# Modulations of two modules as elementwise sums in the feed-forward stage, scan projections spaced by a table, attention without bias tiles

## The chip, the core and the metric

The program runs on one core of a Trainium2 chip, as one launch. A core has a matrix engine (PE), a vector engine (DVE), an activation engine (ACT), a general engine (POOL) and a queue engine that mostly issues DMAs (SP). Each takes its own instructions strictly in order and waits on semaphores that other engines and DMAs raise; sixteen DMA engines move data between DRAM (HBM) and the on-chip memory. The metric is the device time of one execution in microseconds (us), lower is better. All data are float32.

## The reference, cut to what matters

Two blocks of layers run one after the other on 512 tokens of width 1024. Each of three modules needs six modulation vectors of 1024 numbers (shift, scale and gate, twice), made from one conditioning vector by a 1024 x 6144 matrix:

```python
for i in range(DEPTH):                      # first block: modules "0" and "1" of the kernel
    mod = silu(c) @ ada_w[i] + ada_b[i]     # (6144,), and the same for c_ctx
    sh1, sc1, gt1, sh2, sc2, gt2 = split(mod, 6)
    h = x * (1.0 + sc1) + sh1
    y = rwkv7_mixer(h, ...) if i == 0 else pool_mixer(h, ...)
    x = layer_norm(ALPHA * x + gt1 * y)
    h = x * (1.0 + sc2) + sh2
    y = swiglu(h, w1, w3, w2) if i == 0 else moe_swiglu(h, ...)
    x = layer_norm(ALPHA * x + gt2 * y)
# second block: module "2"
mod = silu(c_2) @ w_ada_2 + b_ada_2
h = h + gate1 * attention(modulate(rms_norm(h), shift1, scale1))   # scores + bias[key - query]
h = h + gate2 * conv_ffn(modulate(rms_norm(h), shift2, scale2))
```

The rwkv7 mixer holds a state per head that is updated token by token in both directions (a scan), first over 256 context tokens, then over the 512. The attention of the second block adds to the score of a query and a key a bias that depends on their distance alone.

## The kernel before, in words

The stages follow each other: features and projections of the rwkv7 mixer, its scan, its output projection with a normalisation, the SwiGLU feed-forward stage (hidden width 2816), the pooling mixer with the router, the expert stage, and the second block (attention, convolutional feed-forward).

A matmul in full precision is made of three. `part` splits a float32 tile into a rounded copy (`wh`, ACT, L166) and the remainder (`wl`, DVE, L167), and `mm3` (L172) multiplies high by high, high by low and low by high.

**The scan** (`phase_rwkv`) treats 16 heads as 8 pairs f = 0 to 7. A pair takes three passes of `chain(f, bt)` (L788 to L845): four chunks each, four steps per chunk, in which PE, ACT and DVE hand a 128 x 64 state to each other. `weave` runs a chain step by step and calls `fill` after each step: 48 steps per pair, 384 in all (and 13 before the first). Beside the chain it also runs pieces for the pairs that follow (`gram`, `inv`, `feats1`, `load_k`). `fill` advances the generator `background` by one step. Its steps are of two kinds. One is `job`: projections k, r and v of later pairs, 176 steps with up to six matmuls each (L934), whose results go to DRAM tiles (`kd_`, `rd_`, `vd`) and are read back by `load_k(f)` (L567) and its like. The other is `ada`: a chunk of 1024 columns of a module's modulation, a load of 128 x 1024 weights (512 KB, L228) per step, multiplied on PE with the silu of the conditioning vector as a 32-column stationary operand (L234), nine loads with the bias row, then a tenth step that copies, transposes (L241) and stores. Chunk by chunk, 16 chunks are made there: four of module "0" (its first two vectors are made earlier), six of "1", six of "2". They stand between the jobs from the second set of projections on; after the last job the generator goes on with the chunks that are left in 12 of 16 steps (`SPARE`). `bias_tiles` is called once per pair from the third on: a DMA that writes, for two bias heads, 128 shifted copies of a bias row (`k.bd`) into a DRAM tile `k.zd`.

**The feed-forward stage** (`phase_ffn`) goes over 22 blocks of 128 hidden columns in three groups of 8, 8 and 6 (`FCH`). For each pair of blocks two weight tiles of 1 MB are loaded (`load_w`, L154, four buffers `w`); for each block `glu` splits two 128-column parts of them (three buffers for `wh` and `wl`) and issues 2 x 24 matmuls. After a group `down` multiplies with `ffn_w2`, 192 matmuls for the first two groups; the last group's are spread over the pooling units that follow. Loads of weights are issued by SP, in order.

**Attention** reads for each of 12 bias heads a 128 x 896 tile `zr` from `k.zd` (`zload`, L1835), splits it and adds it to the scores by two matmuls with the identity `identr`.

The order of instructions on each engine is not that of the code: a scheduler places each instruction where its own timeline finds it ready, keeping the dependences. `tc.issue_after` ties a fill to the chain step before it.

## Time and profile before

| | |
|---|---|
| Time, median of 3 runs | 3094.28 us (3085.50 to 3096.80) |
| Profiled execution | 3069.05 us, its span 3067.3 us |
| Busy in the span | PE 2688.0 us (88%), DVE 1479.5 (48%), ACT 1154.6 (38%), POOL 689.6 (22%) |
| DMA | mean 158 GB/s, 484 MB in 334791 packets |
| Granted PE clock | mean 0.907 |

The profile is of one execution, which was some 0.8% quicker than the median of the runs. "Busy" counts the time in which an engine executes; waits and the issuing of DMAs are not in it. The scan lies between about 200 and 1135 us, the output projection up to 1276, the feed-forward stage from 1276 to about 1640. The granted clock is a share of full speed: 1.0 is 2.4 GHz, 0.5 is 1.2 GHz, values between are means over a stretch.

### The profile page before, as it was taken

Reading aid. Unit: us, or ns where it says so; the run is one execution under the profiler, and the core shown is the slowest. Engines: PE = TensorE matmul, PEld = TensorE weight load, DVE = VectorE, ACT = ScalarE, POOL = GpSimd, SP = SyncE. Lnnn points to the kernel's source line nnn. Section 1 sums busy time; section 2 is a strip of 40 time slices with the busy share of each in tenths; the row PEclk is TensorE's granted clock in tenths of the full one; section 3 lists DMA queues with packets and bytes.
Section 4 is the critical chain, followed back from the end, with each engine's and each line's share of the span. In section 5 each row is a group of like instructions: output and inputs, shape, how many; then the busy total and the mean of one; then the engine's idle time right before and its main releaser. Section 6 shows DMA issues by size and latency. Waiting matters only on the chain. (4 is left out here: it accounts for less than half of the span.)

```text
span 3067.3 us, 49827 instructions
## 1 busy us (share of the span) xinstructions
PE 2688.0 (88%) x20336; PEld 2110.3 (69%) x20336; DVE 1479.5 (48%) x2355; ACT 1154.6 (38%) x2163; POOL 689.6 (22%) x827
## 2 busy tenths in 40 slices
PE   5878997978987956799998899999958989989999
PEld 3667665656665644588887787887846855778887
DVE  5876655546565533434346532101146458554544
ACT  5644544536544432322232331111124267343422
POOL 2354444425344322100004300000023200112120
PEclk7888987879887877899999899999988989999999
DMA  7575656646666533323321867888872211222321
GB/s 254 177 222 162 184 179 209 194 150 202 222 191 183 169 124 132 95 96 96 96 69 63 286 198 231 260 275 284 274 264 92 68 40 61 74 83 83 110 86 66
DMA packets 334791, 483.53 MB, mean 158 GB/s; under 512 B 44811, under 2 KB 241692, under 8 KB 327900
## 3 DMA queue, kind: packets, MB, share of 16 engines
q1 hardware_dynamic: 316364, 410.30, 41.2%
q0 software_dynamic: 10992, 60.32, 6.0%
q10 hardware_dynamic: 7200, 9.67, 0.9%
q8 instruction: 162, 2.65, 0.4%
q14 instruction: 73, 0.59, 0.1%
HBM read 424.85 MB, written 60.89 MB: 158 GB/s over the span
## 5 line engine op out<-in xcount | busy, mean ns | idle before, releaser
L167 DVE TENSOR_TENSOR wl<-w,wh 128x1024 fp32r<-128x1024 f32 (+1 forms) x271 | 316.1, 1174 | 517.2 <-ACT wh L166 514.9
L166 ACT CAST wh<-w 128x1024 fp32r<-128x1024 f32 (+1 forms) x271 | 256.5, 955 | 682.1 <-PE mm L172 536.9
L172 PE MATMUL mm<-act,wh 128*128 128x512 f32 x1408 | 437.2, 392 | 12.4 <-ACT act L166 12.4
L172 PEld LDWEIGHTS mm<-act,wh 128*128 128x128 f32 x1408 | 266.4, 189 | 68.4 <-ACT act L166 12.6
L172 PE MATMUL mm<-act,wl 128*128 128x512 f32 x704 | 275.1, 391 | 0.0
L172 PE MATMUL mm<-wh,act 128*128 128x512 f32 x816 | 262.1, 400 | 7.7 <-ACT wh L166 4.1
L172 PEld LDWEIGHTS mm<-wh,act 128*128 128x128 f32 x816 | 157.0, 193 | 47.4 <-ACT wh L166 7.1
L1180 DVE TENSOR_TENSOR silu<-silu,mm 128x512 f32<-128x512 f32 (+4 forms) x77 | 35.4, 459 | 278.6 <-PE mm L1176 183.1
L172 PE MATMUL mm<-wl,act 128*128 128x512 f32 x408 | 163.0, 399 | 3.0 <-DVE wl L167 3.0
L172 PEld LDWEIGHTS mm<-act,wl 128*128 128x128 f32 x704 | 133.0, 189 | 27.8
L234 PE MATMUL bg<-w,cT 128*32 128x256 f32 x1024 | 95.5, 438 | 51.3 <-DMA w<-in_ada_w_dram 39.6
L754 DVE STREAM_TRANSPOSE XT<-T 128x512 f16<-128x512 f16 x120 | 84.7, 706 | 113.5 <-ACT T L752 113.4
L747 DVE TENSOR_TENSOR W<-pW,masks 128x512 f16<-128x512 f32 x120 | 81.7, 681 | 105.5 <-PE pW L745 97.5
L256 POOL DMA_DIRECT2D bc<-gate x6 | 3.6, 605 | 548.9 <-DVEq L1660 529.7
L698 POOL TENSOR_TENSOR GA<-GA,masks 128x512 f32<-128x512 f32 (+1 forms) x96 | 97.2, 1022 | 111.3 <-ACT GA L697 109.0
L694 PE MATMUL gm<-kr,bk 64*128 64x128 f32 (+1 forms) x768 | 117.2, 330 | 2.0 <-DVE kk L600 1.2
L694 PEld LDWEIGHTS gm<-kr,bk 64*128 64x128 f32 x768 | 100.4, 228 | 23.0 <-issue 13.0
L805 POOL TENSOR_TENSOR SP<-S,pc 128x64 f32<-128x64 f32 x176 | 72.2, 427 | 192.3 <-DVE S L845 179.5
L1176 PEld LDWEIGHTS mm<-moxh,w 128*128 128x128 f32 x704 | 105.0, 190 | 7.8 <-issue 5.9
L1176 PE MATMUL mm<-moxh,w 128*128 128x192 f32 (+1 forms) x704 | 107.8, 314 | 2.2 <-DMA w<-in_moe_w_dram 2.1
L752 ACT CAST T<-pT 128x512 f16<-128x512 f32 x120 | 69.9, 583 | 86.6 <-PE pT L750 85.4
L1096 POOL TENSOR_SCALAR bnrs<-bnag 128x1 f32<-128x1 f32 x16 | 6.1, 384 | 419.3 <-DVE bnag L1092 418.9
(511 smaller groups left out, 6219.1 us busy)
## 6 DMA issues: line engine op xcount, KB each, us to landing
w<-in_moe_w_dram SPq DMA_DIRECT2D x109, 1024.0 KB
w<-in_ada_w_dram SPq DMA_DIRECT2D x80, 512.0 KB
w<-in_ffn_w_dram SPq DMA_DIRECT2D x32, 1024.0 KB
w<-in_w_ada_dram SPq DMA_DIRECT2D x48, 512.0 KB
w<-in_w_up_dram SPq DMA_DIRECT2D x22, 1024.0 KB
x<-xdk POOLq DMA_DIRECT2D x18, 1024.0 KB, 5.8
x<-xdv POOLq DMA_DIRECT2D x18, 1024.0 KB, 5.7
w<-in_rk_w_rkv_dram SPq DMA_DIRECT2D x28, 512.0 KB
```

The source lines that it names most:

```text
L166: self.nc.scalar.copy(out=hi, in_=x)
L167: self.nc.vector.tensor_tensor(out=lo, in0=x, in1=hi.bitcast(F32), op=OP.subtract)
L172: self.nc.tensor.matmul(ps, x, y, start=start and i == 0, stop=stop and i == 2, skip_group_check=True)
L234: x = nc.tensor.matmul(ps[32 * j:32 * j + 32, :n], lhsT, rhs[:, j * n:(j + 1) * n], start=(k == 0), stop=(k == 8), tile_position=(0, 32 * j))
L694: nc.tensor.matmul(pss[par][:, s2, d, :nc_], bkj(d, par, j), KR[d][PR(par), j::12, :][:, :nc_ // 64, :], start=True, stop=True)
L698: nc.gpsimd.tensor_tensor(out=out, in0=out, in1=gm, op=OP.mult)
L747: nc.vector.tensor_tensor(out=W16, in0=pW, in1=lmask[:, li, None].to_broadcast(sh), op=OP.mult)
L752: nc.scalar.copy(out=T16, in_=pT)
L754: nc.vector.transpose(fl(XT), fl(T16))
L805: nc.gpsimd.tensor_tensor(out=SP[:, d], in0=S[:, d], in1=PC[d][:, j:j + 1].to_broadcast([128, 64]), op=OP.mult)
L1176: nc.tensor.matmul(ps[:, :n], w[:, kk], xT[:, kk, :n], start=(kk == 0), stop=(kk == KB - 1))
L1180: nc.vector.tensor_tensor(out=s[:, :n], in0=s[:, :n], in1=pss[1][:, :n], op=OP.mult)
```

## The change

The chunks of modules "1" and "2" leave the scan. `ada_sum` makes them in the feed-forward stage instead, in chunks of 512 columns: for each of 8 row blocks a 128 x 512 load (256 KB, four buffers `ws`) is scaled row by row with the conditioning vector and added to an accumulator (three of them, in a free tile of the pool `act`). For module "1" one DVE instruction does both; for module "2" ACT scales and POOL adds. The sum over the 128 rows follows on PE, two chunks later: for shifts and scales four matmuls with the sum as stationary operand and two columns of ones, for gates one matmul of 512 columns, a copy and a store from ACT's queue. `phase_ffn` advances these generators after each block: once after the first block of a pair and twice after the second up to block 16, then once per block. All of the sums end within the stage. The folding of module "1"'s columns, the router's set-up and its gate now follow the stage in the code.

`fill` no longer advances once per step: `PACE` is a table of points (chain step, steps of the generator done by then), 217 in all over 384 steps. Projections come as late as step 268, module "0"'s four chunks after them. `bias_tiles` and `k.zd` go; `zload` reads the shifted rows straight from `k.bd` with rising offsets, and the identity is mirrored to match.

```diff
@@
-SPARE = (1, 5, 9, 13)
+PACE = ((-13, 0), (0, 13), (28, 25), (60, 33), (76, 49), (124, 73), (140, 89), (156, 97), (172, 113),
...
@@
+    def ada_sum(self, room, psp, sp, row, w, b, name, on_pool, n=512):
+        nc = self.nc
+        self.mods[name] = self.vec.tile([128, 48], F32, name="mod" + name)
+        self.gates[name] = [self.dr.tile([1, D], F32, name=f"gate{name}{i}") for i in range(2)]
+        ones = self.c["ones"]
+        room = room.rearrange("p t d -> p (t d)")
+        ws, accs, (bias,) = ([room[:, (o + j) * n:(o + j + 1) * n] for j in range(m)] for o, m in ((0, 4), (4, 3), (7, 1)))
+        def rows_sum(c0, acc):
+            q, r = divmod(c0, D)
+            ps = self.t(psp, [128, 512], tag="mm")
+            if q in (2, 5):
+                nc.tensor.matmul(ps[0:32, :n], ones[:, 0:32], acc, start=True, stop=True)
+                st = self.t(sp, [128, 512], tag="silu")[0:1, :n]
+                nc.scalar.copy(out=st, in_=ps[0:1, :n])
+                nc.scalar.dma_start(out=self.gates[name][q // 3][:, r:r + n], in_=st)
+                return
+            for j in range(n // 128):
+                nc.tensor.matmul(ps[:, 2 * j:2 * j + 2], acc[:, j * 128:(j + 1) * 128], ones[:, 0:2], start=True, stop=True)
+            nc.vector.tensor_copy(self.mods[name][:, c0 // 128:(c0 + n) // 128], ps[:, 0:2 * n // 128:2])
+        pend = []
+        for i, c0 in enumerate(range(0, 6 * D, n)):
+            acc = accs[i % 3]
+            nc.sync.dma_start(out=bias[0:1], in_=b[None, c0:c0 + n])
+            for kk in range(8):
+                wt, c = ws[kk % 4], self.cT[:, kk, row:row + 1]
+                nc.sync.dma_start(out=wt, in_=w[kk * 128:(kk + 1) * 128, c0:c0 + n])
+                if on_pool:
+                    nc.scalar.activation(out=wt, in_=wt, func=AF.Copy, scale=c)
+                    nc.gpsimd.tensor_tensor(out=acc, in0=wt, in1=acc if kk else bias, op=OP.add)
+                else:
+                    nc.vector.scalar_tensor_tensor(out=acc, in0=wt, scalar=c, in1=acc if kk else bias, op0=OP.mult, op1=OP.add)
+            pend.append((c0, acc))
+            if len(pend) > 2:
+                rows_sum(*pend.pop(0))
+            yield
+        for x in pend:
+            yield
+            rows_sum(*x)
+        yield
@@
         def background():
-            adas = seq(ada(0, a["ada_w"][0], a["ada_b"][0], "0", 2 * D, 6 * D), ada(0, a["ada_w"][1], a["ada_b"][1], "1", 0, 6 * D),
-                       ada(2, a["w_ada_2"][0], a["b_ada_2"][0], "2", 0, 6 * D))
             for p in range(1, 4):
                 for n_, lat in (("k", True), ("k", False), ("r", True), ("v", False), ("v", True)):
-                    if (n_, p) == ("r", 1):
-                        continue
-                    yield from job(n_, p, lat)
-                    if p > 1:
-                        yield from next(adas)
-            spare.clear()
-            spare.extend(SPARE)
-            for x in adas:
+                    if (n_, p) != ("r", 1):
+                        yield from job(n_, p, lat)
+            for x in ada(0, a["ada_w"][0], a["ada_b"][0], "0", 2 * D, 6 * D):
                 yield from x
-        spare = []
         mods = background()
+        slot = [PACE[0][0], 0]
         def fill(n):
-            if n % 16 not in spare:
-                next(mods, None)
+            slot[0] += 1
+            for (s0, n0), (s1, n1) in zip(PACE, PACE[1:]):
+                if s0 < slot[0] <= s1:
+                    while slot[1] * (s1 - s0) < n0 * (s1 - s0) + (slot[0] - s0) * (n1 - n0):
+                        slot[1] += 1
+                        next(mods, None)
@@
             with tc.issue_after(uv[0].ins):
                 k.rows.clear(f)
-                if f > 1:
-                    bias_tiles(k, 2 * f - 4)
@@
-def phase_ffn(k, hT, xres, gate2, psp, sp, gp, act):
+def phase_ffn(k, hT, xres, gate2, psp, sp, gp, act, side):
@@
         for f in range(f0, f1, 2):
             w1, w3 = (k.load_w(a[n_][0][:, f * 128:(f + 2) * 128]) for n_ in ("ffn_w1", "ffn_w3"))
-            glu(k, psp, sp, hT, NT, w1, w3, lambda i, s: k.part_to(*g[f - f0 + i], s))
+            def out(i, s):
+                k.part_to(*g[f - f0 + i], s)
+                for _ in range(1 + i if f < 16 else 1):
+                    next(side, None)
+            glu(k, psp, sp, hT, NT, w1, w3, out)
@@
+    for _ in side:
+        pass
     w = [k.t(act, [128, nf, 512], F32R, tag="act") for _ in range(2)]
@@
     k.bd = k.dr.tile([12, 1024], F32, name="biasrows")
-    k.zd = k.dr.tile([12, 128, 896], F32, name="biastiles")
@@
-def bias_tiles(k, h):
-    k.nc.sync.dma_start(out=k.zd[h:h + 2], in_=bass.AP(tensor=k.bd.tensor, offset=k.bd.offset + 1024 * h + 127, ap=[[1024, 2], [-1, 128], [1, 896]]))
@@
-        nc.scalar.copy(out=identr, in_=k.ident)
+        nc.scalar.copy(out=identr, in_=k.ident[:, ::-1])
@@
         def zload(h):
             z = k.t(zr, [128, 896], tag="zr")
-            nc.sync.dma_start(out=z, in_=k.zd[h])
+            nc.sync.dma_start(out=z, in_=bass.AP(tensor=k.bd.tensor, offset=k.bd.offset + 1024 * h, ap=[[1, 128], [1, 896]]))
@@
             gate0 = k.bcast(bc, k.gates["0"][1])
-            m1 = k.mods["1"]
-            G, _ = fold_cols(k, lng(0, 1)[0], None, m1[:, 8:16], None, "1p")
-            cols1 = fold_cols(k, *lng(1, 0), m1[:, 32:40], m1[:, 24:32], "1a")
             rtp = e1.enter_context(tc.tile_pool(reuse_waits="tile", name="rtp", bufs=1))
-            rt, rows = Router(k, rtp, psp, *cols1), k.rows
             with tc.tile_pool(reuse_waits="tile", name="plp", bufs=1) as pp, tc.tile_pool(reuse_waits="tile", name="ffg", bufs=1) as gp:
+                free = tok()
+                nc.gpsimd.memset(free[:, 3], 0.0)
+                side = (x for g in (k.ada_sum(free, psp, sp, 0, a["ada_w"][1], a["ada_b"][1], "1", False),
+                                    k.ada_sum(free, psp, sp, 2, a["w_ada_2"][0], a["b_ada_2"][0], "2", True)) for x in g)
+                block, room = phase_ffn(k, hT, xres, gate0, psp, sp, gp, act, side)
+                m1 = k.mods["1"]
+                G, _ = fold_cols(k, lng(0, 1)[0], None, m1[:, 8:16], None, "1p")
+                cols1 = fold_cols(k, *lng(1, 0), m1[:, 32:40], m1[:, 24:32], "1a")
+                rt, rows = Router(k, rtp, psp, *cols1), k.rows
                 gate1 = k.bcast(bc, k.gates["1"][0])
                 psc = k.bcast(sp, a["pool_scale"], "rsq")
                 nc.vector.tensor_tensor(out=gate1, in0=gate1, in1=psc, op=OP.mult)
-                block, room = phase_ffn(k, hT, xres, gate0, psp, sp, gp, act)
```

On SP, in the scan: the store of the context part of k for the second pair of heads' projections (`kd_`, tiles `st`) and the load `kT` that reads it back for pair f = 2. `UV` are loads for the chain, `w` weights of a job. Before:

```order
L290 DMA kd__72<-st_2325 128x256
L918 DMA w_2920<-in_rk_w_rkv_dram 128x4x256
L290 DMA kd__72<-st_2332 128x256
L687 DMA UV_2579<-vd 64x4x64 x4
L918 DMA w_3235<-in_rk_w_rkv_dram 128x4x256
L555 DMA st_3068<-in_rk_w_dram 64x2x128 x2
L320 DMA vd<-st_2664 128x2x256
L555 DMA st_3068<-in_rk_a_dram 64x2x128 x2
L918 DMA w_3475<-in_rk_w_rkv_dram 128x4x256
L567 DMA kT_3089<-kd__72 128x768
```

and now:

```order
L619 DMA rT_3543<-rd__73 128x512
L1768 DMA w_3453<-in_conehot_dram 32x512
L1769 DMA w_3453<-in_clogm_dram 12x512
L335 DMA kd__72<-st_2709 128x256
L1768 DMA w_3596<-in_conehot_dram 32x512
L1769 DMA w_3596<-in_clogm_dram 12x512
L612 DMA kT_2926<-kd__72 128x768
L335 DMA kd__72<-st_2716 128x256
```

The load `kT` stood seven rows behind the last store; now it stands directly between the two stores.

On DVE, where the first group's blocks end and its `down` begins: `wl` are remainders of weights, `silu` and `gl` the block's output, in the change `act_14236` the accumulators and loads of module "1", `mod` the copy of a row sum from PE. Before:

```order
L167 TENSOR_TENSOR wl_15568<-w_15565,wh_15567 128x1024
L167 TENSOR_TENSOR gl_2365_15040<-silu_15493,gh_2364_15039 128x512
L167 TENSOR_TENSOR wl_15596<-w_15565,wh_15595 128x1024
L1180 TENSOR_TENSOR silu_15556<-silu_15556,mm_15527 128x512
L167 TENSOR_TENSOR wl_15626<-w_15623,wh_15625 128x1024
L167 TENSOR_TENSOR gl_2365_15040<-silu_15556,gh_2364_15039 128x512
L167 TENSOR_TENSOR wl_15654<-w_15623,wh_15653 128x1024
L167 TENSOR_TENSOR wl_15700<-w_15697,wh_15699 128x1024
L167 TENSOR_TENSOR wl_15728<-w_15697,wh_15727 128x1024
```

and now:

```order
L288 SCALAR_TENSOR_TENSOR act_14236<-act_14236,cT 128x512 x4
L1220 TENSOR_TENSOR silu_14976<-silu_14976,mm_14947 128x512
L275 COPY mod_14309<-mm_14998 128x4
L168 TENSOR_TENSOR wl_15092<-w_15089,wh_15091 128x1024
L168 TENSOR_TENSOR gl_2219_14241<-silu_14976,gh_2218_14240 128x512
L288 SCALAR_TENSOR_TENSOR act_14236<-act_14236,cT 128x512 x9
L275 COPY mod_14309<-mm_15021 128x4
L288 SCALAR_TENSOR_TENSOR act_14236<-act_14236,cT 128x512
```

Between the third and the fourth part of the `down` weights the queue now holds the last sums of module "1" (21 of 96, of which nine stand in one row), and the copy of the row sums of its tenth chunk stands between them; on PE these row sums stand ahead of the first `down` matmul.

On POOL, from the last normalisation before the feed-forward stage into it: `xres` is the residual, `bc` the broadcast of a gate, `act_14236` the sums of module "2". Before:

```order
L1108 TENSOR_TENSOR xres<-rsq_14946,bg_14524 128x1024
L1109 TENSOR_TENSOR xres<-xres,bb_14526 128x1024
L256 DMA bg_17035<-in_ln_g_dram 128x1024
L256 DMA bb_17037<-in_ln_b_dram 128x1024
L256 DMA bc_17634<-gate_6904 128x1024
L1096 TENSOR_SCALAR bnrs_17106<-bnag_17102 128x1
L1097 TENSOR_TENSOR bnrs_17106<-bnrs_17106,mhalf 128x1
L1098 TENSOR_TENSOR bnrs_17106<-bnrs_17106,bnnm_17104 128x1
```

and now:

```order
L1149 TENSOR_TENSOR xres<-xres,bb_13765 128x1024
L301 DMA bg_16922<-in_ln_g_dram 128x1024
L301 DMA bb_16924<-in_ln_b_dram 128x1024
L301 DMA bc_16917<-gate_14310 128x1024
L286 TENSOR_TENSOR act_14236<-act_14236 128x512 x12
L301 DMA bc_17521<-gate_14311 128x1024
L286 TENSOR_TENSOR act_14236<-act_14236 128x512 x84
```

The broadcast of module "1"'s second gate, for which POOL waits until the gate is stored, used to stand ahead of the next stage's work; now 12 of 96 additions stand before it and 84 behind it.

## Rows read from the trace of the kernel before

**Rows 1.** Stretches: length, busy PE, PEld, DVE, ACT, POOL, clock, DMA share, GB/s

```profile
200.00:1135.00 935.00, 794.77 (x10842) 587.07 (x10841) 526.13 (x855) 447.21 (x988) 379.03 (x543) 0.84 0.56 177
...
1276.00:1640.00 364.00, 363.67 (x1597) 298.46 (x1597) 143.37 (x172) 94.64 (x113) 16.14 (x18) 1.00 0.26 81
```

**Rows 2.** The same view, one row per pair of heads in the scan

```profile
612.00:751.00 139.00, 111.00 (x1418) 79.72 (x1418) 71.62 (x118) 60.56 (x134) 48.11 (x71) 0.81 0.54 172
...
973.00:1078.00 105.00, 88.94 (x1407) 60.59 (x1406) 56.15 (x94) 45.23 (x107) 39.40 (x60) 0.82 0.54 166
1078.00:1135.00 57.00, 32.38 (x629) 24.56 (x628) 22.84 (x46) 19.05 (x50) 14.55 (x32) 0.79 0.20 64
```

**Rows 3.** PE in the last pair: start, length, instruction, idle before

```profile
1102.73 1.07 PE L234 MATMUL bg<-w,ctile 1*32 1x256 f32 x8 [17.91 <-DMA w<-in_b_ada_dram]
...
1126.03 0.33 PE L788 MATMUL y<-S,kr 64*64 64x64 f32 x4 [0.52 <-DVE S L845]
...
1129.50 0.33 PE L788 MATMUL y<-S,kr 64*64 64x64 f32 x4
```

**Rows 4.** PE waits, 200 to 1135 us: waiter, releaser, us, times, longest

```profile
PE bg L234 <- DMA w<-in_ada_w_dram: 39.6, 15, 13.0
PE bg L234 <- DMA w<-in_b_ada_dram: 17.9, 1, 17.9
PE bg L234 <- DMA w<-in_w_ada_dram: 11.7, 10, 7.7
```

**Rows 5.** Stretch around that wait, columns as in rows 1

```profile
1088.00:1109.00 21.00, 6.27 (x62) 4.63 (x62) 2.47 (x6) 2.00 (x5) 2.56 (x6) 0.51 0.09 36
```

**Rows 6.** PE groups, 200 to 1135 us: busy, mean ns, idle before

```profile
L234 PE MATMUL bg<-w,cT 128*32 128x256 f32 x1024 | 95.5, 438 | 51.3 <-DMA w<-in_ada_w_dram 39.6 <-DMA w<-in_w_ada_dram 11.7
...
L234 PE MATMUL bg<-w,ctile 1*32 1x256 f32 x128 | 11.5, 432 | 17.9 <-DMA w<-in_b_ada_dram 17.9
...
L241 PE MATMUL gm<-ctile,ast 128*128 128x128 f32 x32 | 8.3, 348 | 1.0 <-DVE ast L238 1.0
```

**Rows 7.** Waits of the SP queue at loads of 448 KB

```profile
SPq L1835 <- DMA zr<-biastiles: 31.9, 11, 3.1
```

**Rows 8.** DMA issues by line: tensor, queue, count, KB each

```profile
biastiles<-biasrows SPq DMA_DIRECT2D x6, 896.0 KB
zr<-biastiles SPq DMA_DIRECT2D x12, 448.0 KB
```

**Rows 9.** Answer on tile zh: of those who waited for it, PE's

```profile
  PEld mm L1860: 3.1, 2
```

**Rows 10.** PE: the f32 matmuls nearest to the added ones

```profile
248.22 1.05 PE L295 MATMUL gm<-ctile,st 128*128 128x2 f32 x8
...
1111.90 1.13 PE L898 MATMUL gm<-sg,g 128*128 128x512 f32 x2 [0.16 <-ACT yn L889]
```

**Rows 11.** Groups of DVE, 1150 to 1640 us, shapes apart

```profile
L167 DVE TENSOR_TENSOR wl<-w,wh 128x1024 fp32r<-128x1024 f32 x71 | 86.6, 1225 | 145.4 <-ACT wh L166 143.8
...
L167 DVE TENSOR_TENSOR gl<-silu,gh 128x512 fp32r<-128x512 f32 x22 | 15.0, 683 | 0.0
...
L1268 DVE SCALAR_TENSOR_TENSOR xres<-xres,silu 128x512 f32<-128x512 f32 x16 | 10.6, 685 | 4.5 <-DMA xres<-in_x_dram 4.4
```

**Rows 12.** Groups of POOL and of ACT with 128x512 f32 in SBUF

```profile
L1959 POOL TENSOR_TENSOR cu<-cu,cu 128x512 f32<-128x512 f32 x22 | 28.4, 1293 | 234.7 <-ACT cu L1958 234.7
...
L1958 ACT ACTIVATE cu<-cu 128x512 f32<-128x512 f32 x22 | 13.9, 633 | 44.6 <-DVE cu L1948 44.6
```

**Rows 13.** 50 us of the feed-forward stage, columns as in rows 1

```profile
1300.00:1350.00 50.00, 50.00 (x222) 41.41 (x221) 16.18 (x17) 14.10 (x18) 0.00 (x0) 1.00 0.35 110
```

**Rows 14.** Last stage: three POOL additions and a DVE subtraction

```profile
2832.61 4.80 POOL L1967 TENSOR_TENSOR xres<-silu,xres 128x512 f32<-128x512 f32 x3
...
2834.91 1.35 DVE L167 TENSOR_TENSOR wl<-w,wh 128x1024 fp32r<-128x1024 f32 x1 [0.27 <-ACT wh L166]
```

**Rows 15.** The stretch with the most GB/s, columns as in rows 1

```profile
2200.00:2250.00 50.00, 46.77 (x379) 42.34 (x378) 9.58 (x25) 10.54 (x27) 0.00 (x0) 1.00 0.92 303
```

More of the change, by code (lines that the diff above doesn't have):

```diff
@@ L30 @@
 DECAY = float(np.exp(-0.5))
-SPARE = (1, 5, 9, 13)
+PACE = ((-13, 0), (0, 13), (28, 25), (60, 33), (76, 49), (124, 73), (140, 89), (156, 97), (172, 113),
+        (220, 137), (236, 153), (252, 161), (268, 177), (384, 217))
 POOLM = (1, 3)
```

## The prediction

> **What bounds the kernel now.** I read the view of stretches first. In the scan, PE is busy 794.8 of 935 us, DVE 526 and ACT 447; no other engine is near its limit, and 140.2 us of PE are idle [rows 1]. Pair by pair a stretch takes 105 to 139 us, and 57 once little background is left [rows 2]. The state chain alone is shorter: in the last pair, when PE had nothing else, one chunk followed another after 1129.50 − 1126.03 = 3.5 us [rows 3], and 12 chunks per pair make 42 us. So the scan is set by the sum of PE's work, pieces and background together, and work taken off PE there should shorten it, down to some 60 us per pair.
>
> The view of waits splits the idle time: 39.6 + 17.9 + 11.7 = 69.2 us are waits for the weights of modulations, 71 us all others [rows 4]. One wait of 17.9 us stands in the last pair, and the stretch round it ran at a granted clock of 0.51, the lower of the two levels [rows 3, 5].
>
> The feed-forward stage is the opposite: PE is busy 363.67 of 364 us at clock 1.00, DVE 143, ACT 95, POOL 16, and DMA moves 81 GB/s [rows 1]. DVE, ACT and POOL have room; on PE every added matmul costs its length, and every wait too.
>
> **The change: the scan.** It loses 12 of 16 chunks. Their PE groups cost 95.5 + 11.5 + 8.3 = 115.3 us [rows 6]; three quarters are 86.5. Some of it was overlapped by neighbours' records, so I take 80 (bounds 70 and 86.5). Of the waits, four of the ten ada_w chunks stay (module "0"), 0.4 × 39.6 = 15.8, so 69.2 − 15.8 = 53.4 us go.
>
> Two things come back. The background now has 217 steps for 384 points instead of 336, so a third of the points where PE could fill a wait of the chain have nothing to give. If the other 71 us of idle time grow by that third, it is +24; bounds 0 (the jobs alone cover it) and 71 (it doubles). Second, SP's order shows that the load `kT` for pair f = 2 comes between the stores of the projections it reads, not rows behind them: a late store now delays the chain, and behind this load the queue's other loads. There are five such places; at 0 to 3 us each, the landing of a 448 KB load [rows 7] being the upper one, 0 to 15, and I take 5. Scan: −80 − 53 + 24 + 5 = −104, bounds −140 (no give-back) and −37 (70 and 53 gained, 71 and 15 given back).
>
> **Bias tiles.** Six DMAs of 896 KB go [rows 8], beside PE work in the scan. The twelve loads `zr` keep their 448 KB and change their source; SP waits 2.9 us for one (31.9 / 11) [rows 7], and PE waited 3.1 us in all for the tile made from it [rows 9]. I take 0; −3 if those waits go, +6 if each of the twelve lands half a us later and none is hidden.
>
> **The feed-forward stage.** Row sums on PE: 16 groups of four matmuls with a 128 x 128 float32 operand and two columns. The nearest row has four of this shape, two records each, in 1.05 us; 16 × 1.05 = 16.8. Eight gate sums are like the row of one matmul with 512 float32 columns, 1.13 us [rows 10], together 9.0. PE was full, so +26 without cover; the lower bound, 13, supposes that neighbours overlap half of it, as records in the scan overlap.
>
> Module "1" gives DVE 96 additions, 0.685 us each [rows 11], 66 us beside 143 of 364: room in the mean. The place that counts is the end of the first group of blocks, which DVE's order shows. The row sums of the tenth chunk stand on PE ahead of the first `down` matmul; they need sums that stand on DVE behind the split `wl` of a third weight part, and that part waits for a buffer freed by the last block's matmuls. Late by then: a rounding on ACT (taken as long as the split), the split, 1.22 [rows 11], `gl` 0.68 [rows 11] and nine or so sums, of which six are not covered, 6 × 0.685 = 4.1, less 1 us of matmuls that PE still has, as I take it: 1.22 + 1.22 + 0.68 + 4.1 − 1 = 6 us. Bounds: 0 (the part comes earlier) and 25 (two chunks in line, 16 × 0.685, and both splits after it).
>
> Module "2" has 96 ACT scalings, near 0.633 us, and 96 POOL additions, near 1.293 us [rows 12], 124 us of a POOL that had 16. But POOL's order puts a wait among them: 12 additions, then the broadcast of module "1"'s second gate, which exists only after some block 10, then 84 more. A block is 48 matmuls at 50.00 / 222 = 0.225 us [rows 13], 10.8 us. From 6 us after block 10 to the end of block 16 there are some 66 us for 44 additions whose sums PE wants by then; alone they take 44 × 1.293 = 56.9.
>
> They are not alone. An addition on POOL beside the split `wl` on DVE grew: three took 4.80 us, two of them at about 1.25 and the third over 2.29, since `wl` (1.35 us) began at 2834.91 and the three ended at 2837.41 [rows 14]. Twelve splits and six `gl` in that stretch add about 12 × 1.0 + 6 × 0.5 = 15 us, so 72 instead of 66: +6 (bounds 0, and 44 × 2.29 − 66 = 35 if every addition collides).
>
> The Trainium skill says the same of the mechanism ("SBUF — State Buffer", Who interferes with whom): a DVE instruction with two inputs in SBUF and a POOL instruction that reads SBUF shut each other out for the whole instruction. By it the sums of module "1" would collide as well, which speaks for the upper bound; the trace agrees with the exclusion in the one triple above.
>
> Smaller: a second wait for weight parts in the second `down`, +3; the start, 12 additions in DVE's and POOL's way, less the two broadcasts and `plw` that leave it, +2; clock that falls after such waits, as it did to 0.51 round the 17.9 us one [rows 5], +5 (0 to 12). Feed-forward: 26 + 6 + 6 + 3 + 2 + 5 = +48, bounds 13 (the smallest row sums alone) and 103 (26 + 25 + 35 + 3 + 2 + 12). The router's set-up only moves behind the stage: 0.
>
> **Sum.** −104 + 0 + 48 = −56 against the profiled execution of 3069, which gives 3013. The median of the runs lies 25 us above that execution; I carry that: 3094.3 − 56 = 3038.
>
> **Rivals.** *A, everything is hidden.* The scan gains its full 140 and the stage costs only the row sums, 26: −114, 2980. For: DVE and POOL have room in the mean [rows 1]. Against: the dead points of the fill table and the two ordered places above.
>
> *B, the scan gives only its stalls back.* If the chain and its latencies, not PE's sum, set the pace, the matmuls removed leave idle time and only 53 go: −53 + 48 = −5, 3089, no change. For: PE's idle share of 15% is spread over all pairs, and the clock in the scan is 0.84 [rows 1]. Against: 57 us for the last stretch [rows 2].
>
> *C, slower: the ring of four loads.* The added weights come in 256 KB loads, four buffers, each freed only when its sum is made. Module "1" needs 80 loads by the end of block 8, some 20 of them before the stage: 60p in 86.4 us less nine 1 MB tiles, which at 303 GB/s [rows 15] take 3.46 each, so it stalls 60p − 55. Module "2" needs 44 in 66 us less six tiles: 44p − 45. With p from bandwidth, 262144 B / 303 GB/s = 0.87 us, both are below zero, no stall. But a 448 KB load landed in 2.9 us [rows 7], 1.5 by bandwidth and 1.4 fixed; with one in the air at a time p = 0.87 + 1.4 = 2.25, and 104p − 100 = 134 us of stalls meet −104 + 26: +56, 3150. It decides from p = 1.7 us.
>
> The Trainium skill speaks for C ("DMA: Bandwidth & Descriptors", Bandwidth): it wants transfers of 1 MiB or more for most of the peak. No row here shows a ring of 256 KB loads.
>
> **How the numbers follow.** Main case 0.53, with its own range 3005 to 3075; A 0.18; B 0.15; C 0.14. A measurement here can tell about 0.5%, 15 us, from no change: 3079 and 3110. Faster takes A, nearly all of the main case and a fifth of B: 0.74. Same takes the rest of B and the main case's edge: 0.13. Slower is C less its mildest part, 0.13. The range goes from 2965, just past A, to 3105, past B and into C; about 2 in 10 lie outside.
>
> **What would show it.** In the scan, the groups of modulation matmuls should keep a quarter of their 1024 and 128 instructions, the waits for `w_ada` and `b_ada` should be gone, and the stretches per pair fall by some 13 us in the mean; if they stay while PE's busy share drops, it was B. In the feed-forward stage PE should wait ahead of the row sums at the ends of the first and second group, for DVE first and then for POOL, some 5 to 8 us each, and POOL's additions should average between 1.3 and 1.8 us. Waits of PE or DVE that end with a DMA of the added weights at each chunk are C. The prediction is wrong if the stage grows by under 13 or over 103 us, or if the scan shortens by less than 37.

## The result and the profile after

The changed kernel takes 3043.61 us (median of 4 runs, 3034.05 to 3045.37) beside 3095.54 us of the kernel before: ratio 0.9843, interval [0.9817, 0.9869], 52 us less. Run again later it took 3037.4 us beside 3084.23, ratio 0.9858 [0.9807, 0.991].

The two traces differ by less: the profiled executions took 3069.05 and 3043.58 us, 25.5 us apart. The rest goes with the granted clock, though not strictly. The profiled execution of before had a mean of 0.907; in later comparisons its runs lay between 0.892 (3102.6 us) and 0.906 (3073.4 us), with one of 3061.5 us at 0.905. The changed kernel's lay between 0.894 and 0.902, its profiled one at 0.900. So its profile stands for its runs, and that of before is a quick one: it lies 8 to 15 us below the medians of the three later comparisons (3077.5, 3084.2 and 3079.0 us).

The view of stretches, scan and feed-forward stage of the kernel after (columns as in rows 1: length, busy PE, PEld, DVE, ACT, POOL, clock, DMA share, GB/s):

```profile
200.00:1042.00 842.00, 738.48 (x9916) 582.95 (x9916) 514.03 (x824) 441.62 (x988) 370.22 (x524) 0.83 0.43 130
1184.00:1617.00 433.00, 397.94 (x1758) 321.26 (x1757) 236.44 (x292) 162.92 (x216) 162.55 (x114) 0.95 0.56 179
```

Against [rows 1] the scan is 93 us shorter: PE's busy time fell by 56.3 us and its idle time from 140.2 to 103.5, by 36.7. The waits for the modulations' weights, 69.2 us before [rows 4], are all gone, so the rest of PE's idle time grew from 71.0 to 103.5 us. Its largest single wait is now one for DVE in a piece for later pairs; before and after:

```profile
PE gm L662 <- DVE t L659: 8.1, 5, 3.4
```

```profile
PE gm L707 <- DVE t L704: 25.4, 10, 4.1
```

The feed-forward stage is 69 us longer: PE idles 35.1 us where it idled 0.3, and is busy 34.3 us more: 26.1 for the row sums, 2.0 for the router's set-up (L1374), which now lies in the stage, and some 6 for matmuls that ran slower. What follows moves by some 2 us.

The groups of the modulation matmuls left in the scan, which answer to [rows 6], have no idle time before them:

```profile
L235 PE MATMUL bg<-w,cT 128*32 128x256 f32 x240 | 23.5, 448 | 0.0
L235 PE MATMUL bg<-w,ctile 1*32 1x256 f32 x24 | 1.9, 386 | 0.0
```

PE's waits in the feed-forward stage (waiter, releaser, us, times, longest), and the groups of what was added, with the splits beside them (busy, mean ns, idle before):

```profile
PE mm L274 <- DVE act L288: 16.4, 3, 9.1
PE mm L274 <- POOL act L286: 15.0, 1, 15.0
PE mm L268 <- POOL act L286: 1.4, 1, 1.4
PE mm L173 <- DVE wl L168: 1.2, 1, 1.2
```

```profile
L274 PE MATMUL mm<-ctile,act 128*128 128x2 f32 x128 | 17.9, 263 | 31.4 <-DVE act L288 16.4 <-POOL act L286 15.0
L268 PE MATMUL mm<-act,ctile 128*32 128x512 f32 x16 | 8.2, 603 | 1.4 <-POOL act L286 1.4
...
L286 POOL TENSOR_TENSOR act<-act 128x512 f32<-128x512 f32 x96 | 142.7, 1491 | 139.7 <-ACT act L285 75.5 <-PE mm L268 38.3 <-ACT wh L167 20.6
L168 DVE TENSOR_TENSOR wl<-w,wh 128x1024 fp32r<-128x1024 f32 x63 | 89.9, 1429 | 112.7 <-ACT wh L167 112.0
L288 DVE SCALAR_TENSOR_TENSOR act<-act,cT 128x512 f32<-128x512 f32 x96 | 74.7, 784 | 25.4 <-DMA act<-in_ada_w_dram 23.8 <-DVE act L288 0.3
...
L168 DVE TENSOR_TENSOR gl<-silu,gh 128x512 fp32r<-128x512 f32 x22 | 23.3, 1059 | 0.3 <-ACT gh L167 0.3
```

The row sums take 17.9 + 8.2 = 26.1 us, and 32.8 us of waits stand before them, half for DVE and half for POOL. POOL's additions average 1.49 us where the row of before had 1.29 [rows 12]; beside them `wl` grew from 1.23 to 1.43 and `gl` from 0.68 to 1.06 [rows 11]. While module "2" is made (1364 to 1560 us), POOL also waits for ACT's scalings, and ACT for the loads:

```profile
POOL act L286 <- ACT act L285: 20.2, 14, 3.6
```

```profile
ACT act L285 <- DMA act<-in_w_ada_dram: 62.7, 53, 4.3
```

### The profile page after: what moved, and what is told of

It is laid out like the page before. It is cut to its first block, busy times and chain, and to the rows that moved or that the text cites. A ratio compares the mean times of both kernels' runs of the same rounds, so it can differ in the third digit from the quotient of the medians.

```text
span 3041.8 us, 49004 instructions
## 1 busy us (share of the span) xinstructions
PE 2665.8 (88%) x19592; PEld 2127.8 (70%) x19592; DVE 1562.1 (51%) x2443; ACT 1218.2 (40%) x2267; POOL 826.3 (27%) x908
## 5 line engine op out<-in xcount | busy, mean ns | idle before, releaser
L168 DVE TENSOR_TENSOR wl<-w,wh 128x1024 fp32r<-128x1024 f32 (+1 forms) x271 | 332.1, 1232 | 473.6 <-ACT wh L167 472.4
L286 POOL TENSOR_TENSOR act<-act 128x512 f32<-128x512 f32 x96 | 142.7, 1491 | 139.7 <-ACT act L285 75.5
L850 POOL TENSOR_TENSOR SP<-S,pc 128x64 f32<-128x64 f32 x176 | 59.2, 355 | 194.3 <-DVE S L890 183.0
L285 ACT ACTIVATE act<-act,cT 128x512 f32<-128x512 f32 x96 | 67.6, 723 | 81.6 <-DMA act<-in_w_ada_dram 81.4
```

Of the source, the lines that this page charges most:

```text
L168: self.nc.vector.tensor_tensor(out=lo, in0=x, in1=hi.bitcast(F32), op=OP.subtract)
L285: nc.scalar.activation(out=wt, in_=wt, func=AF.Copy, scale=c)
L286: nc.gpsimd.tensor_tensor(out=acc, in0=wt, in1=acc if kk else bias, op=OP.add)
L850: nc.gpsimd.tensor_tensor(out=SP[:, d], in0=S[:, d], in1=PC[d][:, j:j + 1].to_broadcast([128, 64]), op=OP.mult)
```

## The experiments

All but after_again change the kernel after, and all ran beside the kernel before. Three of them leave work out, so that the router sees other numbers and the expert stage, whose work depends on them, may run far longer (4883 us for scan_only, 4911 for no_loads); they are compared up to the pooling mixer. The table gives two stretches from each trace: from the start of the first matmul of the chains to the end of the last one (L788 before, L833 after), and from there to the first matmul of the pooling mixer (L1294, L1341).

| run | median us | ratio to before | scan chains | to the pooling mixer |
|---|---|---|---|---|
| before | | | 961.8 | 467.9 |
| after | 3043.6 | 0.9843 [0.9817, 0.9869] | 869.2 | 536.7 |
| after_again | 3037.4 | 0.9858 [0.9807, 0.991] | 872.2 | 535.0 |
| scan_only | | | 872.2 | 471.4 |
| fill_dense | 3048.8 | 0.992 [0.9889, 0.9952] | 873.7 | 539.0 |
| gate_late | 3030.1 | 0.9869 [0.983, 0.9907] | 867.2 | 530.1 |
| no_loads | | | 861.8 | 513.3 |
| sums_in_down | 3049.9 | 0.9893 [0.9852, 0.9934] | 865.5 | 551.9 |
| ring5 | 3028.0 | 0.9835 [0.9788, 0.9882] | 863.1 | 532.3 |
| all_dve | 3011.5 | 0.9781 [0.9736, 0.9826] | 867.2 | 515.6 |
| fold_late | 3038.9 | 0.9863 [0.9835, 0.9891] | 877.5 | 534.4 |
| dve_fold_late | 3009.8 | 0.9766 [0.9746, 0.9787] | 871.1 | 515.4 |
| bias_tiles | 3076.2 | 0.9997 [0.9975, 1.0018] | 907.5 | 533.4 |
| scan_less | | | 859.3 | |

Kernels whose scan has the same instructions differ there by up to 16 us (861.8 to 877.5), so that a scan difference below that shows nothing.

**scan_only**: no sums.

```diff
-side = (x for g in (k.ada_sum(free, ...), k.ada_sum(free, ...)) for x in g)
+...                 # sets k.mods["1"], ["2"] and their gates to zeros
+side = iter(())
```

> The changed kernel without the elementwise sums, their loads and their row sums: modules 1 and 2 get vectors of zeros, so the router and the expert stage see other numbers, and the comparison is made up to the end of the feed-forward stage. My theory: the scan keeps its 842 us of the changed kernel (93 less than before) and the feed-forward stage loses all that was added to it, 26 us of row sums on PE, 34 us of waits for sums, about 9 us at its start and in clock: some 66 us less, about 2978 us in all, if the later stages stay. Rival: a part of those 69 us comes from elsewhere (the moved router set-up, the new order in the scan): then the stage shortens by less than 50 and the time stays above 2994.

The stage takes 471.4 us, 65.3 less than after and 3.5 more than before. My theory holds: the stage's growth is the sums and what waits for them; the moved router set-up costs at most a few us.

**fill_dense**: the table of points out.

```diff
-            slot[0] += 1
-            for (s0, n0), (s1, n1) in zip(PACE, PACE[1:]):
-                ...
+            next(mods, None)
```

> The table of points goes: fill advances the background at every chain step again, until its 217 steps are used up. My theory: with the background gone early the last pairs of heads have nothing to fill PE's waits with, so the scan grows by 10 to 25 us, about 3060 us. Rival: PE's sum of work decides, wherever it stands, and the spacing is worth nothing: within 5 us of the changed kernel's 3044.

The scan takes 873.7 us, inside the spread of equal scans. The rival holds for the scan: steps taken without pause and then none cost no more there than steps that are spaced. The median is 5 us above the first of the two medians of the changed kernel and 11 above the second, so that some us elsewhere are not ruled out.

**gate_late**: POOL's broadcast behind the additions.

```diff
+                    self.last_add = nc.gpsimd.tensor_tensor(out=acc, in0=wt, ...)
...
+            with tc.issue_after(k.last_add.ins):
+                gate2 = k.bcast(bc, k.gates["1"][1], "bc")
```

> The broadcast of module 1's second gate is ordered behind the last of module 2's additions, so that POOL waits for nothing between the 12th and the 13th. My theory: PE's one wait of 15.0 us for POOL's sums near the end of the second group goes with the 1.4 us beside it, and the clock stays up there: 12 to 18 us less, about 3029 us. Rival: the additions are limited by their loads (14 us per chunk of eight whatever POOL waited for), so the wait only moves: less than 5 us.

POOL's waits in the stage, the two that matter:

```profile
POOL act L286 <- ACT act L285: 73.5, 15, 50.0
...
POOL act L286 <- PE mm L268: 38.5, 1, 38.5
```

My theory fell. Nothing but additions stands on POOL there now, and it still waits 38.5 us, as it did 38.3 in the kernel after: for PE's row sum L268, which frees one of the three accumulators. That row sum of module "1" stands on PE behind the first `down`. PE's wait for POOL went from 15.0 to 13.7 us only. The median is 13 us below the first one of the changed kernel and 7 below the second; the stage gives 6.6 us, and the ratio to before (0.9869 beside 0.9843 and 0.9858) shows no gain.

**no_loads**: only the first four loads of each module.

```diff
-                nc.sync.dma_start(out=wt, in_=w[kk * 128:...])
+                if i == 0 and kk < 4:
+                    nc.sync.dma_start(out=wt, in_=w[kk * 128:...])
```

> Of the 192 loads of 256 KB only the first four of each module are made; all later sums read the same four buffers again (so the modulations of modules 1 and 2 are other numbers). My theory: the ring of four loads sets the pace of module 1's sums (1.57 us per load where a sum takes 0.75), so without loads DVE is done long before PE asks and the three waits of PE for DVE, 16.4 us, go; module 2 keeps POOL's wait for the gate, but its additions then run at 1.4 to 1.5 us, so that wait shrinks from 15 to 5 to 10 us. In all 18 to 28 us less, about 3022 us. Rival: DVE's own queue (sums that stand behind a split whose buffer comes late) is the cause: PE's waits for DVE stay at 12 us or more and the time within 10 us of the changed kernel's.

PE's waits for sums in this stage, all of them:

```profile
PE mm L274 <- POOL act L287: 8.8, 1, 8.8
```

The 16.4 us for DVE are gone, the wait for POOL shrank from 15.0 to 8.8, and the stage is 23.4 us shorter, as the theory had it. The loads' pace is part of the cause; DVE's order alone is not. For module "2" too: eight chunks of additions (the second to the ninth) took 102 us, 12.8 us each, where they took 115, 14.4 each, in the kernel after.

**after_again**: the kernel after, for comparison.

> The changed kernel as it is, beside the kernel before on the same chip. Its own runs lay at 3034 to 3045 us and those of the kernel before at 3061 to 3102, so I expect 3043 us and a ratio between 0.980 and 0.992; both theories of the feed-forward stage expect the same.

It came out as expected; its waits repeat (15.0 us for POOL, 13.9 for DVE).

**sums_in_down**: gate_late, and three steps of the sums moved into the first `down`.

```diff
+            if f0 == 0 and hf == 0 and tb > 0:
+                next(side, None)
```

> The broadcast stands behind the additions as in the run gate_late, and module 1's last three row sums stand on PE in the middle of the first group's second matmul (behind its first half) instead of behind it. My theory, new after gate_late: POOL's wait of 38 us was for an accumulator that PE's row sum frees, and that row sum stood behind 192 matmuls; now it ends some 22 us earlier, POOL's wait falls below 20 us and PE's wait of 13.7 us for POOL goes: 10 to 15 us less than gate_late in the stage, about 3018 us. Rival: the additions are too slow in themselves (13 to 14 us per chunk where PE asks every 12), so PE's wait for POOL stays at 8 us or more.

POOL's wait of 38 us is gone, but the rival holds, and more: the steps that follow also come earlier, so PE asks for module "2"'s sums sooner than POOL can make them.

```profile
PE mm L274 <- POOL act L286: 25.8, 3, 15.4
PE mm L274 <- DVE act L288: 14.8, 2, 9.3
```

The stage is 15.2 us longer than after. Module "2"'s pace, 14 us per chunk (from 1370.8 us, eight took 113) where PE asks for one every 12, stayed the same with the earlier start. It is not POOL's alone: eight additions of 1.49 us make 11.9 us, and the rest is POOL's waiting for scalings that wait for loads.

**ring5**: five load buffers.

```diff
-wt, c = ws[kk % 4], ...
+wt, c = ws[nx % 5], ...     # ws + [one more 128 x 512 buffer]
```

> Five buffers for the 256 KB loads instead of four. My theory: the pace of module 1's sums, 1.5 us per load, is a round trip of about 6 us over four buffers; with five it falls to about 1.25 us, chunks take 10 us instead of 12, and PE's waits for DVE fall from 16.4 to under 6 us: about 10 us less, 3033 us. Rival: bytes per us decide (with the other weights some 240 GB/s there): the pace stays at 1.5 us and the waits at 13 to 17 us.

```profile
PE mm L275 <- DVE act L290: 15.8, 2, 11.7
PE mm L275 <- POOL act L288: 15.1, 1, 15.1
```

The waits stay. The median is 9 us below after_again, but the intervals overlap; the stage shows 3 us of it. One more buffer does not lift the pace where it matters.

**all_dve**: module 2's sums on DVE.

```diff
-k.ada_sum(free, psp, sp, 2, ..., "2", True)
+k.ada_sum(free, psp, sp, 2, ..., "2", False)
```

> Module 2's sums go to DVE as well (0.75 us each instead of a scaling on ACT and an addition of 1.49 us on POOL). My theory: the start at 1370 us stays (the accumulator waits for the row sum behind the 192 matmuls), but chunks then take 12 us by the ring instead of 14, so PE's wait at the end of the second group falls from 15 to 2 to 6 us and nothing collides with POOL: 8 to 14 us less, about 3033 us. Rival: DVE's splits of weights, which stand behind sums that wait for loads, come late, so that PE waits for splits instead: within 5 us of the changed kernel or slower.

PE's waits for sums, all of them:

```profile
PE mm L274 <- DVE act L288: 15.2, 3, 9.3
```

The wait for POOL is gone altogether, at the unchanged place of the row sums; the stage is 19.4 us shorter than in after_again, the median 26 us, more than I expected; the runs of the two lie apart (3009 to 3025 and 3032 to 3053 us). With DVE a chunk takes 12.0 us (eight in 96.3). DVE's splits do not come late: the rival falls.

**fold_late** and **dve_fold_late**: the products with module 1's first gate behind its last sum; the second with all_dve as well.

```diff
+                with tc.issue_after(k.last_sum.ins):
+                    nc.vector.tensor_tensor(out=gate1, in0=gate1, in1=psc, op=OP.mult)
...
+                with tc.issue_after(k.last_sum.ins):
+                    pool = Pooling(k, pp, G, gate1, room)
```

> The product of module 1's first gate with the pooling scale, and the eight products that fold it into the pooling weights, are ordered on DVE behind the last sum of module 1. In the changed kernel they stand among the sums of the ninth chunk: DVE waits 4.5 us for the broadcast of that gate and then works 4.4 us on the products. My theory, new from the trace: these 9 us, and not the ring of loads, make the two waits of PE for DVE at the end of the first group (6.9 and 9.1 us): they fall to 4 to 8 us together and the time by 8 to 12 us, to about 3032 us. Rival: the ring of loads sets the pace of the sums and catches up with any gap: the waits stay at 13 us or more.

> As fold_late, and module 2's sums on DVE as in the run all_dve. If the two causes are apart, the gains add: all_dve 3011 less 8 to 12 us, about 3001 us. If they share one (DVE late by the same gap), the time stays within 4 us of 3011.

The trace of after had suggested it: among the last sums that PE waits for, DVE waited for a broadcast and folded a gate into weights.

```profile
1266.36 1.22 DVE L168 TENSOR_TENSOR wl<-w,wh 128x1024 fp32r<-128x1024 f32 x1
1272.05 1.23 DVE L2127 TENSOR_TENSOR bc<-bc,rsq 128x1024 f32<-128x1024 f32 x1 [4.48 <-DMA bc<-gate]
1273.19 0.75 DVE L288 SCALAR_TENSOR_TENSOR act<-act,cT 128x512 f32<-128x512 f32 x1
1273.85 3.25 DVE L1331 SCALAR_TENSOR_TENSOR plw<-plw,fs1p,bc 128x256 f32<-128x256 f32 x8
```

With these moved away, PE's two waits are

```profile
1287.65 1.05 PE L274 MATMUL mm<-ctile,act 128*128 128x2 f32 x8 [0.96 <-DVE act L288]
1300.70 1.84 PE L274 MATMUL mm<-ctile,act 128*128 128x2 f32 x8 [12.00 <-DVE act L288]
```

The first fell from 6.9 to 1.0, the second grew from 9.1 to 12.0, and DVE's waits for loads just before (1195 to 1304 us) are 22.9 us against 17.2 (1195 to 1300) in the kernel after: the loads took the gap back. Neither kernel is faster than the one without the move (ratios 0.9863 beside 0.9858, 0.9766 beside 0.9781). The sums keep the pace of the SP queue and its loads together: in the kernel after, the 40 sums before the chunk with the products took 59.4 us (1206.3 to 1265.7), 1.49 us each, and with that chunk 48 took 78.9 us, 1.64 each. Five buffers and this move together were not tried.

**bias_tiles**: the tiles written and read as before.

```diff
+                if f > 1:
+                    bias_tiles(k, 2 * f - 4)
...                 # bias_tiles, k.zd and identr as in the kernel before
-in_=bass.AP(tensor=k.bd.tensor, offset=k.bd.offset + 1024 * h, ap=[[1, 128], [1, 896]])
+in_=k.zd[h]
```

> The changed kernel with the tiles of the attention's bias written to DRAM in the scan again (six DMAs of 896 KB) and read from there. My theory: these DMAs lie beside PE's work and the loads are hidden either way: within 6 us of the changed kernel's 3040 us, the attention 0 to 4 us shorter, the scan 0 to 4 us longer. Rival: the stores fill the queues in the scan and hold up the chain's loads: the scan is 8 us or more longer.

This is the run that the prediction needed. The six DMAs cost all of the change's gain: 3076.2 us, ratio 0.9997 [0.9975, 1.0018] to the kernel before, where fold_late, in the same comparison, has 3038.9 us and 0.9863. The chains take 35 us more than in after_again and 30 more than in the slowest of the equal scans. In the view of stretches PE is busy as long as in after_again (745.2 us from 199 to 1047), but idle for 882.0 − 745.0 = 137.0 us instead of 102.8, nearly as before the change (140.2):

```profile
198.00:1080.00 882.00, 745.02 (x9949) 588.26 (x9949) 518.32 (x824) 442.32 (x991) 373.45 (x527) 0.81 0.42 131
...
713.50:726.50 13.00, 0.00 (x0) 0.00 (x0) 0.00 (x0) 1.15 (x4) 0.00 (x0) 0.50 0.34 115
```

The second row is one of its holes, in which nearly everything stands still. There are three, of 13.4, 13.1 and 8.0 us, which end 22 to 29 us behind the first, third and sixth issue of bias tiles; their 34.4 us account for the 34.2 by which PE is idle longer. SP (SPq: it issues DMAs), ACT and PE around the second:

```profile
697.96 1.82 SPq L1762 DMA_DIRECT2D biastiles<-biasrows  x1
707.35 18.92 SPq L335 DMA_DIRECT2D kd__72<-st  x2
```

```profile
725.31 0.58 ACT L334 COPY st<-bg 128x512 f32<-128x512 f32 x1 [12.68 <-DMA kd__72<-st]
```

```profile
726.53 0.69 PE L833 MATMUL ch<-UV,BT 128*64 128x64 f32 x8 [13.07 <-ACT UV L871]
```

A store `kd_` issued behind the bias tiles does not land, ACT waits for its buffer, and `UV` of the chain is queued behind ACT's copy. The same pattern stands in the kernel before: SP's queue, and the gap of PE behind it,

```profile
606.95 0.65 SPq L1747 DMA_DIRECT2D biastiles<-biasrows  x1
607.70 8.47 SPq L228 DMA_DIRECT2D w<-in_ada_w_dram  x1
616.27 0.25 SPq L231 DMA_DIRECT2D w<-in_ada_b_dram  x1
616.63 14.21 SPq L918 DMA_DIRECT2D w<-in_rk_w_rkv_dram  x2
```

```profile
629.32 1.08 PE L234 MATMUL bg<-w,cT 128*32 128x256 f32 x8 [13.04 <-DMA w<-in_ada_w_dram]
```

Five gaps of 4.5 to 17.9 us that ended with weights of a modulation, 51 of the 69.2 us of [rows 4], begin 3 to 24 us behind an issue of bias tiles (at 483, 607, 859, 968 and 1082 us; the one at 750 has no such gap); the last is the wait of 17.9 us in [rows 3]. What the DMA engines did from 1082 to 1103 us of before, in 40 slices (busy share in tenths, then GB/s), and the row of the view of stretches from 1086 to 1100:

```profile
DMA  9996212111111111111111111111111111111100
GB/s 348 348 341 174 53 37 86 41 55 55 55 55 55 55 41 55 55 55 55 55 41 55 55 55 55 55 55 41 55 55 55 55 55 48 48 55 55 55 21 0
```

```profile
1086.00:1100.00 14.00, 0.00 (x0) 0.00 (x0) 0.00 (x0) 0.00 (x0) 0.00 (x0) 0.58 0.13 53
```

A busy share of 0.13 at 53 GB/s: few of the sixteen engines carry the 896 KB, which by this take 917504 B / 53 GB/s = 17 us. Behind them SP issued one row of 4 KB (`b_ada`). The issue alone took 8.3 us from 1082.4 on, where SP's issues take 0.4 us in the median, and PE waited for the row until 1102.7, when the share had fallen to nothing. At 607 us SP was held too (8.47 us above); then two loads of 512 KB were issued by 617.3 us. The share from 617 to 627 us:

```profile
DMA  5955989999998732111111011111011111011111
```

Most of both loads had moved by 621 us (1.18 MB from 616 on), yet PE waited for the first until 629.3. So what is issued behind the tiles on the same queue seems to wait with the part that it has on the tiles' engines; no view here names the single engines. The Trainium skill has the rule ("DMA: Bandwidth & Descriptors", Why a DMA increments its semaphore by 16 and not by 1): a transfer is spread over the largest number of engines up to 16 that divides the outermost dimension of its patterns. Here that dimension is 2, one for each head; 2 / 16 is an eighth, and the trace's 0.13 agrees.

**scan_less**: module 0's chunks left out too.

```diff
-            for x in ada(0, a["ada_w"][0], a["ada_b"][0], "0", 2 * D, 6 * D):
-                yield from x
+            nc.vector.memset(k.mods["0"][:, 16:48], 0.0)
+            ...         # and zeros into its gates
```

> The changed kernel without module 0's four chunks in the scan (its last four vectors are zeros, so the later stages see other numbers; compared up to the end of the scan's chain). Theory: PE's sum of work sets the scan, so 27 us of PE work less shorten it by 12 to 25 us, as 86 us less gave 93 with the waits for weights. Rival: the chain and its latencies set it since the change: less than 6 us, PE's idle time grows instead.

The scan takes 859.3 us, 10 less than after, 13 less than after_again; PE is busy 720.7 us, 18 less. That leans to the theory, but equal scans differ by as much, and this is a single run: it settles little.

## Why the prediction was right or wrong

The time, 3038 us, was met (3043.6), the direction too. By the stretches of the two traces the scan gave −93 for −104 forecast, and the stage +69 for +48; the whole gave −25.5 for −56. The number was met in part by luck: I had carried the 25 us between the profiled execution and the median of before over to the changed kernel, which does not have them. How much of the 30 us is error is open, as the trace of before is a quick one; by the medians the change took 52 and 47 us off.

*What bounds the scan.* PE's sum of work holds as far as the runs go: with the tiles kept (bias_tiles) PE's idle time is that of before, within 4 us, while PE's busy time fell by 50 us and the chains got 54 us shorter. In the change itself PE's busy time fell by 56.3 us, less than the 80 that I took and the lower bound of 70. Record by record, the time in which PE ran nothing but modulation matmuls fell by 74 us (95.7 to 21.6), inside the bounds; but the other matmuls kept PE busy 18 us longer (699.0 to 716.8 us). Why is open.

*Of the waits 53.4 us go.* All 69.2 went, module "0"'s too. The cause was wrong for the greater part: the trace put them down to the loads of the modulations' weights, which were what PE waited for, but 51 us of them stood behind bias tiles; and bias_tiles, which has module "0"'s loads alone, shows such holes, two of three at the store of a projection instead.

*Bias tiles, 0.* This is the step that failed. "Beside PE work" looked at what the DMAs moved and not at what was queued behind them; they were worth some 35 us in the scan with this kernel's order. What they would be worth in the order of before was not run. With the tiles kept, the change is no gain: by the table −54 us in the scan chains and +66 up to the pooling mixer. So the tiles alone may be the whole of it; the kernel before without them was not tried. The loads `zr` from their new source are worth nothing, as forecast: 3.5 us of waits for the tile made from them, beside 3.1 [rows 9].

*What comes back, +24 and +5.* Right in size: the idle time that is no wait for weights grew from 71.0 to 103.5 us, by 32.5. The cause is not shown: in fill_dense all points without a fill stand at the end, and the scan is no longer; no wait for the load `kT` stands among those of the scan. More than half of it is PE's wait L707 for DVE, 25.4 us for 8.1.

*Row sums, +26.* Right: 26.1.

*The end of the first group, +6, and module "2", +6.* The places were right, and the engines. Both were too small, 16.4 and 16.4 us. (The bound of 25 for the first does not come out of the terms named beside it: 16 × 0.685 and two splits with their roundings make 16.) In the first, I had the split late and not the loads; no_loads shows that without loads the wait goes. In the second, the additions were longer, as forecast (1.49 for 1.29 us); the sums of module "1", which I had thought to collide as well, ended at 1314.8 us, before POOL's first addition. But the wait of POOL that I put down to the broadcast is one for an accumulator (gate_late), and the pace of loads, scalings and additions together decides (no_loads, sums_in_down, all_dve). The moved set-up, costed at 0, put 9 us into DVE's queue at the worst place, which the loads would have taken anyway (fold_late).

*Clock.* Right in kind: 0.95 in the stage instead of 1.00; an estimate of its cost is some 6 of the 34.3 us by which PE is busier (34.3 − 26.1 − 2.0), where I took 5. The 2.0 us are the router's matmuls, which I had costed at 0.

*Rivals.* A fell with the waits in the stage, B with PE's idle time in the scan, which did not grow as PE's work left. C was partly there: for module "1" a 256 KB load came every 1.49 to 1.64 us, under the 1.7 from which C was to decide, and the waits that it made for PE were 16 us, not 130.

## What to carry to other kernels

A wait "for a load" can be a wait for what was issued ahead of it on the same queue: look at what SP issued just before each gap, and at the DMA share in it, before crediting the gap to the load that ended it. Here a share of 0.13 while the queue was full was a transfer on few engines. When work moves into a stage whose bound engine is full, price what asks for it (one chunk every 12 us) against what makes it (14 by ACT and POOL, 12.0 on DVE): starting earlier did not help here, where PE also asked earlier; a faster engine did; with all sums on DVE the kernel takes 3011.5 us, ratio 0.9781 [0.9736, 0.9826], faster than both kernels.

## What was unexpected of the hardware

Runs of one kernel on one chip spread by 1.3% with the granted clock: the kernel before took 3061.5 us at 0.905 and 3102.6 at 0.892. A comparison of two single profiles carries that spread.
